# Mixers of a hybrid diffusion trunk: half-filled products on TensorE widened to 128 rows or 128 columns

## Chip, cores and metric

The kernel runs on one core of one Trainium2 chip. The metric is the device time of one execution in microseconds (us), the median over the runs.

## What is computed

One inference step of a trunk with two layers, shared by 512 latent tokens and 128 prompt tokens. Each layer is a half-step FFN, a mixer and a second half-step FFN, each behind an RMS norm with a modulation. The mixer has three parallel groups of heads: MLA (8 heads, softmax over all keys), a sliding window with grouped queries (SWA, 8 query heads on 2 key/value heads, a band of 128 to either side, cached context and a sink), and a gated delta net (GDN, 4 heads, in both directions, a scan over chunks of 64 tokens).

```python
def mixer_latent(h, lp, ctx):
    pr = project_mixers(h, lp)
    o_mla = mla_attend(q_nope, rope(q_rope), [kn_l, kn_c], [rope(krope), krope_c], [v_l, v_c])
    o_swa = swa_band_attend(rope(sq), rope(sk), sv, sk_c, sv_c, sink)
    o_gdn = gdn_bidirectional(pr, lp, st_fwd, st_bwd)
    return concat([o_mla, o_swa, o_gdn]) @ lp['w_out']

def gated_delta_step(s, w_i, u_i, qd_i, kd_i, a_i, gt_i):   # one chunk of 64 tokens
    v_new = u_i - w_i @ s
    o_i = qd_i @ s + a_i @ v_new
    s = s * gt_i + kd_i.T @ v_new                           # state, 128 x 128
```

## The kernel before

Activations lie with features on the partitions and the 640 tokens (512 latent, 128 prompt) along the row. Weighted products are made in float32r: every operand is split into a high and a low part, and a product is hi·hi + lo·hi + hi·lo; the rest of the mixer is in float32, where one product appears in the trace as two passes.

The program is a list of Python calls from which a tile framework makes one fixed order per engine, by a simulated timeline of its own (`schedule_with_timeline_sim`). At run time every engine works its list strictly in that order, and semaphores join the lists. So where the order of two engines isn't changed, a faster engine only meets its next wait earlier.

**Projections and GDN** (`mixer`, L316 on). `linear` (L93 to L108, products at L104) multiplies `h` by the weights of the mixers, three float32r products for each 128 features and each half of the 640 columns. Between these products the framework places the GDN of heads 0 to 3 (`gdn_group`, L592). Within a group, tokens lie in four pairs of chunks (u = 0 to 3), each pair on 128 partitions: chunk c on rows 64c to 64c+63. For each direction d POOL makes `kd` (L665, L666), the keys times the decay to the end of their chunk, `ekd` (from `gates`, L588). `step` (L729 to L740) is one chunk of the scan: L736 multiplies by the state (128 rows), L737 (DVE) puts the new values into the chunk's half of `UU`, and L739 makes the update of the state from that half:

```python
ps = slice(c * 64, c * 64 + 64)
nc.tensor.matmul(p2[:, :P], lhsT=KD_[d][ps, us], rhs=UU[d][ps, us], start=True, stop=True)
```

There are 16 such steps in a group, five groups in a layer (the fifth, for the prompt, is worked beside SWA) and two layers: 160.

**SWA** (`swa`, L939 to L1002). For each key/value head, `kh` (the high part of the keys) is loaded twice, into rows 0 to 63 and 64 to 127; `kl` (the low part) once, into rows 0 to 63; the values `vv` as [128, 6, 64]. `qh` holds the high part of the queries on rows 0 to 63 and the low part on rows 64 to 127. So one product of 128 rows gives hi·hi + lo·hi, and a second one of 64 rows hi·lo:

```python
for lh, rh in ((qh[:, q], kh[:, k0:k0 + w]), (qh[:64, q], kl[:64, k0:k0 + w])):
```

These alternate at L974: for each head four products for the first two blocks of queries, two for each of the others, and two for the prompt (L999). A mask product follows (L978), then `finish` (softmax: DVE, ACT, and POOL for the division, L899 to L909).

**Products with the values** (`pv`, L912 to L937; SWA and MLA). The probabilities are transposed on TensorE (L924), copied by ACT (L931), and multiplied at L935 with the values of one head as weights, 128 rows by 64 columns; the result lies on 64 partitions of PSUM and ACT copies it out (L937). SWA has 9 such products for each head, MLA 11.

**MLA** (`mla`, L1004 to L1043): keys and queries of 96 rows, scores at L1029, `vv` loaded for every head from `dv`, which `project` (L843 to L855) has written as [8 heads, 128, 6, 64]. After the first heads, the finished outputs are read back (`of`, L507) and split for the last product of the mixer.

Of the kernel before, what the change touches and what calls it, by code (L numbers as in the profile page):

```python
# [14 lines left out]
P = 128  # L15
# [26 lines left out]
class Net:  # L42
# [13 lines left out]
    def banks(self, **n):  # L56
        """psum tags and their banks, for the phase that opens"""
        side = {"side": n.pop("side")} if "side" in n else {}
        return _Banks(self, n, self.pool(self.nm("psum"), space=PSUM, reuse_waits="tile", **side))
# [12 lines left out]
    def move(self, dst, src):  # L72
        """between memories, of values that are float32r on either side"""
        raw = lambda x: x.bitcast(F32) if x.dtype == F32R else x
        self.nc.sync.dma_start(raw(dst), raw(src))
# [17 lines left out]
    def linear(self, ws, rhs, m=P, cols=HALVES, after={}):  # L93
        """for each column range: psum[:m, :n] = sum_k w[k]^T rhs[k], in three float32r products."""
        nc = self.nc
        ps = []
        kt = len(rhs)
        for c0, cw in cols:
            p = self.pt("L")
            ps.append(p)  # L100
            for k in range(kt):
                (wh, wl), (rh, rl) = ws[k], rhs[k]
                for n, (w, r) in enumerate(((wh, rh), (wl, rh), (wh, rl))):
                    i = nc.tensor.matmul(p[:m, :cw], lhsT=w[:, :m], rhs=r[:, c0:c0 + cw],  # L104
                                         start=(k == 0 and n == 0), stop=(k == kt - 1 and n == 2))
                    if (k, n) in after:
                        self.tc.add_manual_dep(i.ins, after[k, n].ins.name, mybir.DependencyInfo(mybir.DependencyClass.NoSync, mybir.DependencyReason.DATA), reason="norm")
        return ps  # L108

    def square(self, pool, xk, nfeat, bufs=3):  # L110
        """takes the squares (by the number of features) of one more tile of features"""
        nc = self.nc
        sq = pool.tile([P, T], F32, tag="sq", name=self.nm("sq"), bufs=bufs)
        for c0, cw in HALVES:
            nc.scalar.activation(sq[:, c0:c0 + cw], xk[:, c0:c0 + cw], AF.Square, scale=nfeat ** -0.5)
        self.addsquare(sq)
# [10 lines left out]
    def rstd(self, pool, kind="G", windows=(0, 128, 256, 384, 512), last=True):  # L127
        """by token (partition) and window of 128: 1/sqrt(mean(x^2) + eps) over the features squared so far"""
        nc = self.nc
        nb = len(windows)  # L130
        ps = self.pt(kind)
        r0, r = (pool.tile([P, nb], F32, tag="rs", name=self.nm("rs"), bufs=2) for _ in range(2))
        for i, t in enumerate(self.sq):
            for b, c in enumerate(windows):
                self.lastmm = nc.tensor.matmul(ps[:, 2 * b:2 * b + 2], lhsT=t[:, c:c + P], rhs=self.ones[:, :2],
                                               start=(i == 0 and b == 0), stop=(i == 1 and b == nb - 1))
        if last:
            self.sq = []
        nc.vector.tensor_scalar(r0, ps[:, :2 * nb].rearrange("p (b c) -> p b c", c=2)[:, :, 0], EPS, None, ALU.add)
        nc.gpsimd.tensor_tensor(r, r0, self.mhalf[:, :nb], ALU.pow)  # L140
        return r

    def spread(self, r, half, windows, kind="G"):
        """r [token, window] on every partition, tokens along the row: psum of a column half"""
# [36 lines left out]
    def addgate(self, k, ps, G, sq=None, half=None):  # L181
        """adds to the features k the gated columns of ps, and takes their squares"""
# [10 lines left out]
    def residual(self, k, w, rhs, G, squares):  # L193
        """x[k] += gate * (w^T rhs); after the last k the norm's factors of the first half of the columns
        are worked out beside the products of the second"""
# [52 lines left out]
    def adaln(self, l, i, start=False):  # L248
        """columns i*512 to (i+1)*512 of silu(cond) @ w_ada + b_ada, by feature and group: the sums over the
        blocks of 128 features on the vector engine and GpSimd and the rest on the tensor engine, or all there"""  # L250
# [42 lines left out]
    def fill(self, *after):  # L293
        """a job where the tensor engine has more to do than the others"""
# [5 lines left out]
    def rope(self, pool, z, np_, kind, mask):  # L300
        """rotate the latent columns of z in place"""
# [13 lines left out]
    def mixer(self, l, A, B, G):  # L315
# [17 lines left out]
        def parts(s, m=P, w=T):  # L333
            """hi and lo of s"""
# [4 lines left out]
        def put(d, hl):  # L339
            """latent and prompt columns into [latent, cache, prompt]"""  # L340
# [17 lines left out]
        # gates and the rotary key  # L358
# [9 lines left out]
        # gated delta-net: convolution, silu  # L368
# [6 lines left out]
        def prompt(n, hh, src):  # L375
            """the prompt's columns of a head, kept for the last group"""
# [32 lines left out]
        def window():  # L409
# [11 lines left out]
            # values by token: latent blocks, cache, prompt  # L421
# [126 lines left out]
    def gates(self, l, gp, pg):  # L548
# [9 lines left out]
        # softplus(y) = max(y, 0) + log1p(exp(-|y|)), log1p(e) = 2 atanh(e / (2 + e))  # L558
# [29 lines left out]
        self.egc, self.ekd, self.egt = ex[:, 0:40], ex[:, 40:80], (ex[:, 80:120], ex[:, 120:160])  # L588
# [3 lines left out]
    def gdn_group(self, l, g, qw, k, v, z):  # L592
        """g < 4: the latent tokens of head g, in four pairs of chunks; g == 4: the prompt, a pair of chunks by head."""
# [9 lines left out]
        # norms of k and q by token  # L603
# [22 lines left out]
        # natural layouts  # L626
# [9 lines left out]
        # K K^T and K Q^T  # L636
# [10 lines left out]
        for d in range(2):  # L647
# [17 lines left out]
            kd = t("kd", 3)  # L665
            nc.gpsimd.tensor_tensor(u4(kd), u4(kn), cols(self.ekd, d), ALU.mult)  # L666
            KD_.append(kd)
        # inverses of the 16x16 diagonal blocks of I+U (d=1 transposed: both are upper triangular)
# [57 lines left out]
        # scan over the chunks  # L726
        oq = [t("oq", 3) for _ in range(2)]

        def step(d, S, ci):  # L729
# [9 lines left out]
            nc.tensor.matmul(p2[:, :P], lhsT=KD_[d][ps, us], rhs=UU[d][ps, us], start=True, stop=True)  # L739
# [60 lines left out]
    def project(self, l, st, draw, tab32, pair):  # L800
# [24 lines left out]
        # keys: columns latent, cache, prompt  # L825
# [17 lines left out]
        self.dv = self.dram.tile([8, P, 6, 64], F32, tag=self.nm("dv"), name=self.nm("dv"))  # L843
        for b in range(6):
# [8 lines left out]
            t = cast("hd", [P, 8, 64])  # L853
            nc.scalar.activation(t, p.rearrange("p (h d) -> p h d", d=64), AF.Copy)
# [37 lines left out]
    def finish(self, S, scale, nscale, nsink, sink):  # L892
        """softmax weights of the score columns S [P, parts, columns], by row; scale: a number, or one by row"""
# [18 lines left out]
    def pv(self, blocks, vv, o, r0, c0, width):  # L912
        """blocks: list of (value block, [(probability tile, its column, output block)]);
        o[r0:r0+64, c0:c0+width] = sum over the value blocks."""
# [19 lines left out]
        for n, (vb, ti, s0, w, oc) in enumerate(place):  # L934
            nc.tensor.matmul(po[:64, oc:oc + w], lhsT=vv[:, vb, :], rhs=hl[ti][:, s0:s0 + w],  # L935
                             start=(n == 0), stop=(n == len(place) - 1))
        nc.scalar.activation(o[r0:r0 + 64, c0:c0 + width], po[:64, :width], AF.Copy)  # L937

    def swa(self, l):  # L939
        nc, att = self.nc, self.att  # L940
        sink = self.sm(l, 'sink')
        for kv in range(2):
            # columns: latent, cached context, prompt
            kh, kl = (att.tile([P, 768], F32R, tag="k", name=self.nm("k"), bufs=4) for _ in range(2))
            vv = att.tile([P, 6, 64], F32, tag="vv", name=self.nm("vv"), bufs=2)
# [3 lines left out]
            self.move(kl[:64], self.dsk[1][rows])  # L949
            self.move(vv, self.dsv[kv])  # L950
            for hh in range(4):
# [9 lines left out]
                def scores(n):  # L961
# [10 lines left out]
                    for o0, k0, w in rng:  # L972
                        for lh, rh in ((qh[:, q], kh[:, k0:k0 + w]), (qh[:64, q], kl[:64, k0:k0 + w])):
                            nc.tensor.matmul(p[:, o0:o0 + w], lhsT=lh, rhs=rh, start=(k == 0), stop=(k == last - 1))  # L974
                            k += 1
# [22 lines left out]
                for n, (lh, rh) in enumerate(((qh[:, TL:], kh[:, T:]), (qh[:64, TL:], kl[:64, T:]))):  # L998
                    nc.tensor.matmul(p[:, :P], lhsT=lh, rhs=rh, start=(n == 0), stop=(n == 1))  # L999
# [4 lines left out]
    def mla(self, l, heads, wp=None, osplit=None, hook=None):  # L1004
        nc, a, att = self.nc, self.a, self.att
        for head in heads:
# [12 lines left out]
            vv = att.tile([P, 6, 64], F32, tag="vv", name=self.nm("vv"), bufs=2)  # L1019
            self.move(vv, self.dv[head])  # L1020
            if head % 2 == 0:
                ot = (wp or att).tile([P, T], F32, tag="of" if wp else "out", name=self.nm("of"), bufs=2)
# [125 lines left out]
class _Banks:  # L1148
    """psum tags and their banks, as long as the context lasts"""
# [13 lines left out]
class _Bufs:  # L1163
    """a pool whose tags have their own number of buffers"""
# [38 lines left out]
def _layout(x):  # L1203
    """the inputs, laid out as the tiles that the program loads."""
    C = np.ascontiguousarray

    def tiles(w, k, n):
        """[L, K, N] -> [L, N/n, P, K/P, n]"""
# [9 lines left out]
    # q, k, v, z of the delta-net; sk, sv, sq; ckv, cq  # L1218
# [48 lines left out]
```

## Time and profile before

| | |
|---|---|
| median of 3 runs | 3419.33 us (3416.01 to 3420.2) |
| profiled execution | span 3412.5 us, which is all that the profile gives of its own time |
| runs above the span | 6.8 us |
| TensorE: busy, products / weight loads | 98% / 91% |
| DVE, ACT, POOL busy | 55%, 41%, 13% |
| granted clock, mean | 0.987 |

The span runs from the first to the last instruction of one profiled execution. Busy shares of TensorE are of modelled ends of pipelined products, so that how fast it goes is read from the distance between the starts of its instructions, in the timeline. A layer's mixer stands at 556 to 1246 us and at 2237 to 2925 us; the stages used below are the scans of GDN heads between the projections (to about 912 and 2594 us), SWA with the prompt's GDN group (to 1046 and 2728), and MLA (to 1161 and 2839).

### The profile page before, as it was taken

What the parts mean: (1) busy time and instruction counts of PE and PEld (TensorE: products, weight loads), DVE (VectorE), ACT (ScalarE), POOL (GpSimd) and SP (SyncE); (2) the same over time, 40 slices, a digit from 0 to 9 for tenths busy, and PEclk for the clock granted to TensorE, in tenths of its full rate; (3) what the DMA queues carried; (4) which work ended last, traced back from release to release, by engine and by line L of the source; (5) the groups of instructions that cost most, each with busy time, mean ns of one, the idle gap of its engine ahead of it and who ended that gap; (6) DMA issues with size and microseconds to landing.
All of it is one profiled execution on the core that took longest, in us unless ns stands there. A gap on an engine that the chain in (4) does not pass through costs nothing.

```text
span 3412.5 us, 56739 instructions
## 1 busy us (share of the span) xinstructions
PE 3356.0 (98%) x22036; PEld 3112.9 (91%) x22036; DVE 1880.6 (55%) x4353; ACT 1387.8 (41%) x3041; POOL 429.8 (13%) x460
## 2 busy tenths in 40 slices
PE   8999999999999999999999999999999999999998
PEld 5999999999866799999999999999997668999998
DVE  4574677676765345643346745477777553433333
ACT  3332335544565533322233323264455563322222
POOL 0010011211333200000000100012113341000000
PEclk9999999999999999999999999999999999999999
DMA  5353453222514223432224524323143142222222
GB/s 210 125 156 109 145 167 106 92 74 90 170 45 123 85 87 120 149 107 77 66 90 142 164 97 137 102 86 107 65 130 125 49 136 80 75 71 74 80 67 76
DMA packets 181470, 363.21 MB, mean 106 GB/s; under 512 B 34256, under 2 KB 70736, under 8 KB 181200
## 3 DMA queue, kind: packets, MB, share of 16 engines
q1 hardware_dynamic: 181200, 359.58, 32.9%
q8 instruction: 173, 2.83, 0.3%
q14 instruction: 97, 0.79, 0.1%
HBM read 313.46 MB, written 46.04 MB: 105 GB/s over the span
## 4 chain that ended last, share of the span: by engine, by line
PE 92%; DVE 4%; DMA 2%; ACT 1%; issue 1%; SPq 0%; POOL 0%; POOLq 0%; DVEq 0%; ACTq 0%
PE psL L104 71%; PE psT L935 4%; PE psG L697 3%; PE psT L924 2%; PE psS L739 2%; PE psS L974 2%; PE psS L1029 1%; PE psS L736 1%; PE psG L275 1%; DVE hf L169 1%; DMA of<-do 1%; PE psS L770 1%; PE psL L852 1%; DMA adaw<-in_wada_dram 0%; PE psG L610 0%
## 5 line engine op out<-in xcount | busy, mean ns | idle before, releaser
L70 DVE TENSOR_TENSOR wlo<-wr,whi 128x512 fp32r<-128x512 f32 (+2 forms) x726 | 495.0, 683 | 709.2 <-ACT whi L67 707.2
L67 ACT ACTIVATE whi<-wr 128x512 fp32r<-128x512 f32 (+2 forms) x726 | 446.3, 616 | 883.2 <-PE psL L104 622.2
L104 PE MATMUL psL<-hb,whi 128*128 128x320 f32 x1968 | 523.3, 313 | 1.1 <-DVE hb L171 1.1
L104 PE MATMUL psL<-hc,whi 128*128 128x320 f32 x1952 | 519.4, 313 | 0.4 <-DVE hc L171 0.4
L104 PE MATMUL psL<-ha,whi 128*128 128x320 f32 x1856 | 492.5, 312 | 5.3 <-DVE ha L171 4.0
L104 PE MATMUL psL<-hd,whi 128*128 128x320 f32 (+1 forms) x1856 | 486.8, 310 | 3.5 <-DVE hd L171 3.5
L104 PE MATMUL psL<-mh,wlo 128*128 128x320 f32 x1408 | 434.2, 309 | 0.0
L104 PE MATMUL psL<-ml,whi 128*128 128x320 f32 x1408 | 434.0, 309 | 0.0
L104 PE MATMUL psL<-mh,whi 128*128 128x320 f32 x1408 | 432.9, 310 | 0.0
L104 PEld LDWEIGHTS psL<-hb,whi 128*128 128x128 f32 x1968 | 351.1, 189 | 4.7 <-DVE hb L171 2.3
L104 PEld LDWEIGHTS psL<-hc,whi 128*128 128x128 f32 x1952 | 348.0, 189 | 3.1 <-DVE hc L171 1.0
L104 PEld LDWEIGHTS psL<-ha,whi 128*128 128x128 f32 x1856 | 329.7, 188 | 10.1 <-DVE ha L171 5.9
L104 PEld LDWEIGHTS psL<-hd,whi 128*128 128x128 f32 (+1 forms) x1856 | 328.6, 187 | 8.1 <-DVE hd L171 5.2
L269 DVE SCALAR_TENSOR_TENSOR ada<-adaw,cs,ada 128x512 f32<-128x512 f32 x448 | 313.6, 743 | 0.0
L104 PE MATMUL psL<-hb,wlo 128*128 128x320 f32 (+1 forms) x984 | 307.0, 312 | 0.0
L104 PE MATMUL psL<-hc,wlo 128*128 128x320 f32 (+1 forms) x976 | 305.2, 313 | 0.0
L104 PE MATMUL psL<-hd,wlo 128*128 128x320 f32 (+1 forms) x928 | 287.8, 310 | 0.0
L104 PE MATMUL psL<-ha,wlo 128*128 128x320 f32 (+1 forms) x928 | 287.7, 311 | 0.0
L104 PEld LDWEIGHTS psL<-ml,whi 128*128 128x128 f32 x1408 | 264.0, 188 | 2.8
L104 PEld LDWEIGHTS psL<-mh,whi 128*128 128x128 f32 x1408 | 263.5, 188 | 3.0
L104 PEld LDWEIGHTS psL<-mh,wlo 128*128 128x128 f32 x1408 | 264.1, 188 | 2.0
L188 DVE SCALAR_TENSOR_TENSOR x<-psL,G,x 128x320 f32<-128x320 f32 (+2 forms) x240 | 97.8, 435 | 231.3 <-PE psL L104 231.0
(298 smaller groups left out, 5591.2 us busy)
## 6 DMA issues: line engine op xcount, KB each, us to landing
adaw<-in_wada_dram SPq DMA_DIRECT2D x288, 256.0 KB, 2.9
wr<-in_w1a_dram SPq DMA_DIRECT2D x88, 512.0 KB, 3.6
wr<-in_w1b_dram SPq DMA_DIRECT2D x88, 512.0 KB, 3.5
wr<-in_win_dram SPq DMA_DIRECT2D x54, 512.0 KB, 3.5
wr<-in_w2a_dram SPq DMA_DIRECT2D x32, 512.0 KB, 4.0
wr<-in_w2b_dram SPq DMA_DIRECT2D x32, 512.0 KB, 3.5
wr<-in_wo_dram SPq DMA_DIRECT2D x16, 512.0 KB, 3.6
dqn<-hd SPq DMA_DIRECT2D x24, 320.0 KB, 2.7
```

Source lines behind the costliest of these rows:

```text
L67: self.nc.scalar.activation(dst, src, AF.Copy)
L70: self.nc.vector.tensor_tensor(dst, src, hi.bitcast(F32), ALU.subtract)
L104: i = nc.tensor.matmul(p[:m, :cw], lhsT=w[:, :m], rhs=r[:, c0:c0 + cw], start=(k == 0 and n == 0), stop=(k == kt - 1 and n == 2))
L169: nc.vector.scalar_tensor_tensor(t[:, c0:c0 + n], self.x[k][:, s], A[:, k, g:g + 1], r[j][:, c0:c0 + n], ALU.mult, ALU.mult)
L188: i = self.nc.vector.scalar_tensor_tensor(xs, ps[j][:, c0:c0 + n], G[:, k, g:g + 1], xs, ALU.mult, ALU.add)
L269: nc.vector.scalar_tensor_tensor(acc[g], raw, c, acc[g], ALU.mult, ALU.add)
L275: nc.tensor.matmul(ps[:2, :], lhsT=self.sel[:, g, :], rhs=x, start=(g + n == 0), stop=(g + n == 2))
L697: nc.tensor.matmul(p[:, s], lhsT=lhs[:, s], rhs=rhs[:, s], start=True, stop=True)
L739: nc.tensor.matmul(p2[:, :P], lhsT=KD_[d][ps, us], rhs=UU[d][ps, us], start=True, stop=True)
L924: nc.tensor.transpose(pt[:, used:used + P], pr[:, pc:pc + P], self.ident)
L935: nc.tensor.matmul(po[:64, oc:oc + w], lhsT=vv[:, vb, :], rhs=hl[ti][:, s0:s0 + w], start=(n == 0), stop=(n == len(place) - 1))
L974: nc.tensor.matmul(p[:, o0:o0 + w], lhsT=lh, rhs=rh, start=(k == 0), stop=(k == last - 1))
```

## The change

No product is left that uses only 64 rows or 64 columns in these three places:

- **State update.** `gates` makes two `ekd`, each zero on the rows of the other chunk; POOL makes two `kd` for each direction (buffers 3 to 6), and the update multiplies all 128 rows. The other chunk's rows meet zeros.
- **Scores of SWA.** `kl` is loaded into both halves, and both products have 128 rows. The second one now also adds lo·lo.
- **Values.** In MLA `vv` holds two heads side by side, [128, 6, 128], loaded once for two heads, and `dv` is written as [4, 128, 6, 128]; in SWA both halves are loaded with the same values. The product has 128 columns, and ACT copies out the 64 partitions of its head.

```diff
@@ gates
-        self.egc, self.ekd, self.egt = ex[:, 0:40], ex[:, 40:80], (ex[:, 80:120], ex[:, 120:160])
+        self.egc, self.egt = ex[:, 0:40], (ex[:, 80:120], ex[:, 120:160])
+        self.ekd = []
+        for c in range(2):
+            e = t(f"ekd{c}", 40)
+            nc.vector.tensor_tensor(e, ex[:, 40:80], self.mat[('blka', 'blkb')[c]][:, 0:1].to_broadcast([P, 40]), ALU.mult)
+            self.ekd.append(e)
...
@@ gdn_group
-            kd = t("kd", 3)
-            nc.gpsimd.tensor_tensor(u4(kd), u4(kn), cols(self.ekd, d), ALU.mult)
+            kd = [t("kd", 6) for _ in range(2)]
+            for c in range(2):
+                nc.gpsimd.tensor_tensor(u4(kd[c]), u4(kn), cols(self.ekd[c], d), ALU.mult)
...
-            nc.tensor.matmul(p2[:, :P], lhsT=KD_[d][ps, us], rhs=UU[d][ps, us], start=True, stop=True)
+            nc.tensor.matmul(p2[:, :P], lhsT=KD_[d][c][:, us], rhs=UU[d][:, us], start=True, stop=True)
...
@@ project
-        self.dv = self.dram.tile([8, P, 6, 64], F32, tag=self.nm("dv"), name=self.nm("dv"))
+        self.dv = self.dram.tile([4, P, 6, P], F32, tag=self.nm("dv"), name=self.nm("dv"))
...
-            t = cast("hd", [P, 8, 64])
-            nc.scalar.activation(t, p.rearrange("p (h d) -> p h d", d=64), AF.Copy)
+            t = cast("hd", [P, 4, P])
+            nc.scalar.activation(t, p.rearrange("p (h d) -> p h d", d=P), AF.Copy)
...
@@ pv
-            nc.tensor.matmul(po[:64, oc:oc + w], lhsT=vv[:, vb, :], rhs=hl[ti][:, s0:s0 + w],
+            nc.tensor.matmul(po[:, oc:oc + w], lhsT=vv[:, vb, :], rhs=hl[ti][:, s0:s0 + w],
                              start=(n == 0), stop=(n == len(place) - 1))
-        nc.scalar.activation(o[r0:r0 + 64, c0:c0 + width], po[:64, :width], AF.Copy)
+        nc.scalar.activation(o[r0:r0 + 64, c0:c0 + width], po[r0:r0 + 64, :width], AF.Copy)
...
@@ swa
-            vv = att.tile([P, 6, 64], F32, tag="vv", name=self.nm("vv"), bufs=2)
+            vv = att.tile([P, 6, P], F32, tag="vv", name=self.nm("vv"), bufs=2)
...
-            self.move(kl[:64], self.dsk[1][rows])
-            self.move(vv, self.dsv[kv])
+                self.move(kl[half], self.dsk[1][rows])
+                self.move(vv[:, :, half], self.dsv[kv])
...
-                        for lh, rh in ((qh[:, q], kh[:, k0:k0 + w]), (qh[:64, q], kl[:64, k0:k0 + w])):
-                            nc.tensor.matmul(p[:, o0:o0 + w], lhsT=lh, rhs=rh, start=(k == 0), stop=(k == last - 1))
+                        for x in (kh, kl):
+                            nc.tensor.matmul(p[:, o0:o0 + w], lhsT=qh[:, q], rhs=x[:, k0:k0 + w], start=(k == 0), stop=(k == last - 1))
...
-                for n, (lh, rh) in enumerate(((qh[:, TL:], kh[:, T:]), (qh[:64, TL:], kl[:64, T:]))):
-                    nc.tensor.matmul(p[:, :P], lhsT=lh, rhs=rh, start=(n == 0), stop=(n == 1))
+                for n, x in enumerate((kh, kl)):
+                    nc.tensor.matmul(p[:, :P], lhsT=qh[:, TL:], rhs=x[:, T:], start=(n == 0), stop=(n == 1))
...
@@ mla
-            vv = att.tile([P, 6, 64], F32, tag="vv", name=self.nm("vv"), bufs=2)
-            self.move(vv, self.dv[head])
             if head % 2 == 0:
+                vv = att.tile([P, 6, P], F32, tag="vv", name=self.nm("vv"), bufs=2)
+                self.move(vv, self.dv[head // 2])
```

The number of TensorE's products stays the same, and so does their order up to SWA, but for some transposes and norms that stand a few places from where they stood. From L585 on, lines of the changed kernel are 5 to 7 higher: the update of the state is L745, the scores L981 and L1006, the values L942, `kd` L672.

In each block of rows below, numbers after `_` are the program's own and move with every added tile. The first place is SP's queue at the start of SWA in the first layer; `k` are the two key tiles, `q` the queries of a head, `v` an operand of the prompt's GDN group. Before:

```order
L75 DMA k_10484<-dsk_7256 64x768 x2
L75 DMA k_10485<-dsk_7257 64x768
L75 DMA vv_10486<-dsv_7343 128x384
L478 DMA v_9490<-d_992_5811 128x512
L75 DMA q_10492<-dsq_7503 64x640
L75 DMA q_10492<-dsq_7504 64x640
```

and with the change:

```order
L75 DMA k_10508<-dsk_7268 64x768
L75 DMA k_10509<-dsk_7269 64x768
L75 DMA vv_10510<-dsv_7355 128x6x64
L478 DMA v_9510<-d_994_5815 128x512
L75 DMA k_10508<-dsk_7268 64x768
L75 DMA k_10509<-dsk_7269 64x768
L75 DMA vv_10510<-dsv_7355 128x6x64
L75 DMA q_10518<-dsq_7515 64x640
L75 DMA q_10518<-dsq_7516 64x640
```

Two more loads stand ahead of the first queries.

The second place is TensorE's list at the same point (L736 and L739, now L742 and L745, are the last head's scan; L610 and L629, now L615 and L634, open the prompt's GDN group; L974, now L981, are the first scores). Before:

```order
L736 MATMUL psS_1635_9038<-st_9034,wqb_8455 128x128
L974 MATMUL psS_10495<-k_10484,q_10492 128x256
L974 MATMUL psS_10495<-k_10485,q_10492 128x256
L974 MATMUL psS_10495<-k_10484,q_10492 128x128
L974 MATMUL psS_10495<-k_10485,q_10492 128x128
```

and with the change:

```order
L742 MATMUL psS_1645_9058<-st_9054,wqb_8471 128x128
L615 MATMUL psG_9517<-ones,QK_9518 128x2 x4
L615 MATMUL psG_9517<-ones,QK_9524 128x2 x4
L634 MATMUL psG_9543<-mats,k_9509 128x128 x4
L745 MATMUL psS_1645_9058<-uu_9035,kd_8841 128x128
L981 MATMUL psS_10521<-k_10508,q_10518 128x256
L981 MATMUL psS_10521<-k_10509,q_10518 128x256
```

Thirteen products of GDN now stand ahead of the first scores.

The third place is POOL's list in the scan of head 0, where the second direction's `kd` of head 1 stands (`pad` are the zero borders for a convolution, cleared by POOL). Before:

```order
L388 MEMSET pad_8673 128x2
L388 MEMSET pad_8673 128x4
L388 MEMSET pad_8673 128x2
L666 TENSOR_TENSOR kd_6936<-kn_6878,gex_5793 128x512
L756 MEMSET st_9776 128x128
```

and with the change:

```order
L672 TENSOR_TENSOR kd_6946<-kn_6886,ekd_962_5795 128x512
L672 TENSOR_TENSOR kd_6947<-kn_6886,ekd_963_5797 128x512
L388 MEMSET pad_8689 128x2
L388 MEMSET pad_8689 128x4
L388 MEMSET pad_8689 128x2
L762 MEMSET st_9800 128x128
```

One `pad` is now cleared behind the two `kd`, no longer ahead of the one.

## Rows read from the trace of the kernel before

**Rows 1.** The chain that ended last: share of the span by engine.
```profile
PE 92%; DVE 4%; DMA 2%; ACT 1%; issue 1%; SPq 0%; POOL 0%; POOLq 0%; DVEq 0%; ACTq 0%
```

**Rows 2.** Busy us by stage: stretch and length, PE, PEld, DVE, ACT, POOL, PEclk, DMA.
```profile
660.00:850.00 190.00, 189.58 (x1326) 179.15 (x1325) 130.53 (x364) 89.51 (x218) 35.67 (x50) 0.98 0.25 82
912.00:1046.00 134.00, 133.82 (x742) 92.20 (x742) 84.25 (x331) 82.07 (x253) 46.58 (x53) 0.97 0.20 58
1046.00:1161.00 115.00, 107.89 (x570) 74.19 (x570) 54.99 (x140) 71.79 (x172) 44.53 (x41) 0.94 0.41 125
2594.00:2728.00 134.00, 133.16 (x745) 91.83 (x744) 86.97 (x335) 82.33 (x253) 47.17 (x55) 0.99 0.20 58
2728.00:2839.00 111.00, 104.99 (x569) 72.64 (x569) 56.34 (x140) 71.47 (x172) 44.04 (x41) 0.97 0.43 131
```

**Rows 3.** Busy us of L739 alone ahead of SWA: PE (xpasses), PEld.
```profile
660.00:912.00 252.00, 23.52 (x96) 14.32 (x96) 0.98 0.35 112
```

**Rows 4.** TensorE's timeline around one L739: start us, us, what, xpasses.
```profile
888.90 0.31 PE L104 MATMUL psL<-hb,wlo 128*128 128x320 f32 x1
889.05 0.31 PE L104 MATMUL psL<-hb,whi 128*128 128x320 f32 x1
889.29 0.49 PE L739 MATMUL psS<-uu,kd 64*128 64x128 f32 x2
889.70 0.41 PE L104 MATMUL psL<-hc,whi 128*128 128x320 f32 x1
889.95 0.31 PE L104 MATMUL psL<-hc,wlo 128*128 128x320 f32 x1
```

**Rows 5.** The same view around one L736, of equal shape but 128 rows.
```profile
694.67 0.31 PE L104 MATMUL psL<-hb,whi 128*128 128x320 f32 x1
694.82 0.38 PE L736 MATMUL psS<-st,wqb 128*128 128x128 f32 x2
694.95 0.39 PE L104 MATMUL psL<-hb,whi 128*128 128x320 f32 x1
695.18 0.31 PE L104 MATMUL psL<-hb,wlo 128*128 128x320 f32 x1
```

**Rows 6.** The same view: scores of two blocks of queries, and the masks behind.
```profile
957.43 1.30 PE L974 MATMUL psS<-k,q 128*128 128x384 f32 x4
958.67 0.28 PE L978 MATMUL psS<-bmsw,identb 128*128 128x128 bf16 x2
...
961.05 0.93 PE L974 MATMUL psS<-k,q 128*128 128x512 f32 x2
961.91 0.29 PE L978 MATMUL psS<-bmsw,identb 128*128 128x128 bf16 x2
```

**Rows 7.** The same view in MLA: values (L935) between scores.
```profile
1129.46 1.12 PE L1029 MATMUL psS<-k,q 96*128 96x320 f32 x6
1130.51 1.08 PE L935 MATMUL psT<-pt,vv 128*64 128x256 f32 x4
1131.52 0.33 PE L924 MATMUL psT<-mats,pr 128*128 128x128 f32 x1
1131.60 1.12 PE L1029 MATMUL psS<-k,q 96*128 96x320 f32 x6
1132.65 0.65 PE L935 MATMUL psT<-pt,vv 128*64 128x256 f32 x2
```

**Rows 8.** Groups of weight loads by shape: xcount, busy us, mean ns, idle before.
```profile
L935 PEld LDWEIGHTS psT<-pt,vv 128*64 128x64 f32 x640 | 74.1, 137 | 52.3 <-issue 8.6 <-ACT pt L931 7.6 <-ACT pr L904 1.5
L739 PEld LDWEIGHTS psS<-uu,kd 64*128 64x128 f32 x320 | 46.6, 187 | 26.5 <-issue 8.4 <-ACT pr L904 2.0 <-ACT den L906 1.3
```

**Rows 9.** POOL's groups: `kd`, mean ns of one, and what POOL waited for.
```profile
L666 POOL TENSOR_TENSOR kd<-kn,gex 128x512 f32<-128x512 f32 x20 | 22.0, 1106 | 99.1 <-PE psS L739 82.0 <-ACT bd L704 15.3 <-ACT kn L631 1.8
```

**Rows 10.** SP's timeline: issues of the first SWA keys.
```profile
903.63 1.79 SPq L75 DMA_DIRECT2D k<-dsk  x3
```

**Rows 11.** A piece of the chain in MLA: start us, us, what.
```profile
1074.79 4.73 DMA of<-do
```

## Prediction

> **What bounds the kernel now.** I read the chain of waits first: 92% of it is TensorE's work [rows 1], so every nanosecond taken from TensorE's list counts wherever TensorE doesn't wait. Then the busy times by stage, to see where that holds. While the scans of heads 0 to 3 run between the projections, and in SWA, TensorE is busy for all but a fraction of a microsecond of the stage (189.6 of 190, 133.8 of 134), and DVE and ACT for some 60 to 70% of it; in MLA TensorE falls short of its stage by 6 to 7 us [rows 2]. Busy ends are modelled, though, so the third view is the timeline, where the distance between starts tells what a product costs. Here the three edited products stand out.
>
> *State update.* In a stream of full products (one each 0.15 us, 888.90 to 889.05) the two passes of L739, on 64 rows, start 0.24 us after the product ahead of them. The next full one starts 0.41 us later, and the one after it 0.25 us later: 0.90 us from the last full product ahead to the second behind [rows 4]. L736, of the same kind and columns on 128 rows, passes through the same stream in 0.51 us (694.67 to 695.18) [rows 5]. So the half-height update is the dearer one, by 0.39 us: it is paid when TensorE goes to it, between its own passes, and when it returns.
>
> *Scores.* Four products, in turn of 128 and 64 rows, take 1.24 us (957.43 to 958.67), and a pair of 512 columns 0.86 us [rows 6]. By the column, a full product of 320 columns at 0.15 us [rows 4] gives about 0.24 us for 512 columns and 0.18 for 384 (estimates), and the 128-column ones lie below 0.15.
>
> *Values.* Six scores of 96 rows with 320 columns take 1.05 us between two runs of L935 [rows 7], where six full products at 0.15 would take 0.88 to 0.90. So the price of going to L935's 64 columns and back sticks to its neighbours too, while 96 rows cost nothing extra: six at 0.15 fit but for that price.
>
> **The change part by part.**
>
> *State update, removed cost.* 320 passes [rows 8] are 160 updates. Ahead of SWA there are 96 passes in the first layer [rows 3], and the second layer runs the same program: 96 updates, mostly among full products, at 0.38: 36 us. The other 64 stand in the SWA stage, often beside L935 or L974, where entry and exit are shared; bounds 0.28 (own passes and one edge: 0.41 less 0.13) and 0.39, I take 0.36: 23 us.
>
> *Scores, removed cost.* A set of four goes from 1.24 to about 0.58 (0.18 + 0.18 + 0.11 + 0.11), a saving of 0.66; a pair of 512 from 0.86 to 0.47, a saving of 0.39. For each head there are two sets of four, two long pairs and the prompt's short pair (taken at half a set, 0.33): 2.4 us. Sixteen heads: 38 us. Bounds: with 0.15 for every short product 34, with 0.08 42.
>
> *Values, removed cost.* 640 passes [rows 8], mostly four in a run [rows 7]: some 160 runs. The six scores show 0.15 to 0.17 us of it (one entry and the second product after a return); the exit itself adds about 0.09, by the entry of L739 [rows 4]. I take 0.25 us a run, bounds 0.15 and 0.39: 40 us (24 to 62). With 9 products a head in SWA and 11 in MLA, 18 us of it lie in SWA and 22 in MLA.
>
> *Sum on TensorE:* 36 ahead of SWA, 23 + 38 + 18 = 79 in SWA, 22 in MLA, 137 in all.
>
> *What of it reaches the end.* Ahead of SWA, DVE (130.5 of 190) and ACT have room [rows 2], the order is the same, and TensorE hardly waits: 90%, 33 us. In SWA each layer's 134 us would become 94; DVE has 84 to 87 us of work there and ACT 82 [rows 2], in chains (maximum, exponential, division, transpose, copy) through two PSUM banks for scores and two for the rest. Both at 90% is more than such chains give. I take 72%, 57 us: each stage about 106 us, with DVE and ACT near 80%. What is late next there is a softmax, not a product. In MLA TensorE waits already, and the chain runs through read-backs of finished heads of up to 4.7 us each [rows 11]; half, 11 us.
>
> *What it adds.* Twenty more `kd` on POOL at 1.1 us [rows 9]. POOL is busy 36 of 190 us there [rows 2]; the cover is its idle time. But it waits in order: it has spent 82 us waiting for a scan to release a `kd` buffer [rows 9], and a `pad` now stands behind two such `kd` where it stood ahead of one. That can hold the pad's convolution on DVE, and weights behind it, by one scan step and two `kd`, some 5 us; DVE has room, so I take nothing, bounds 0 and 10 over both layers. At SWA's start two more loads, at 0.6 us to issue [rows 10], stand ahead of the first queries: 1.2 us later in each layer; thirteen GDN products were moved ahead of the scores and cover about that. I take 3 us for both layers with the slower strided load of `vv`, bounds 0 and 7. In MLA eight loads fewer of `vv`, hidden before: nothing. Two small multiplications more on DVE in `gates`: below 1 us, nothing. ACT copies the same 64 partitions: nothing.
>
> *Sum.* 33 + 57 + 11 - 3 = 98 us. The profiled span of 3412.5 us becomes 3314.5; the runs' median lies 6.8 us above the span, so **3321 us**.
>
> **The rivals.**
>
> *Wider weight loads (slower than forecast).* The values' loads go from 64 to 128 columns: 137 ns now, 187 ns for 128 columns [rows 8], 50 ns more for each of 640. If none is hidden, 32 us come back: 3353 us. Against it: L736's two passes, with loads as wide, need 0.13 us to the next product's start [rows 5], less than one load takes, so that loads run under products. The Trainium skill ("TensorE: Matmul & The Clock Gate", LDWEIGHTS) says that the time of a load goes by columns and not by rows; the trace agrees (187 ns on 64 rows, 137 at half the columns), and the rule speaks against the third part of the change alone.
>
> *The others hold the softmax stages.* DVE, ACT and the read-backs set the length of SWA and MLA as soon as TensorE is quicker; only the 33 us ahead of SWA are left: 3386 us. For it: DVE and ACT at 65% in SWA, two banks each. Against it: TensorE waits under 1 us in 134 [rows 2], so the others now run ahead of it.
>
> *The price isn't one of size.* It stays with the products when they are filled, because of the places where they stand or their operands: 3412 to 3426 us, no difference. Against it: L736 stands in the same places and doesn't pay [rows 5]. The Trainium skill ("TensorE: Matmul & The Clock Gate", "Why this matters for your kernels") would come out near here: a product over a few rows takes the same time as one over 128, and small ones only gain by running side by side. By it neither update nor scores would save anything, and the sum would be 24 us from the values, 3395 us. Rows 4 and 5 contradict it for 64 rows: 0.39 us apart.
>
> *Slower: the clock.* The granted clock is 0.94 to 0.99 in the two stages [rows 2], the lowest in MLA, where TensorE waits most. If quicker products turn into waits and the clock falls, all else there is slower. After the gain the stages hold about 106 and 109 us in a layer, 430 in both, at about 0.97. At clock c they need 430 x 0.97 / c: the gain of 98 us is eaten at c = 0.79, and at 0.70 the kernel takes 3321 + 166 = 3487 us. Against it: the clock is 0.97 and more in SWA, with its present chains.
>
> **How the numbers follow.** Forecast 0.77; wider loads 0.08; softmax stages 0.07; no difference 0.04; clock 0.04. The range: all 137 us arrive and nothing is added, 3282, which I cut to 3286, since no stage has ever all of it; at the other end 80% ahead of SWA (29), 40% in SWA (32), nothing in MLA and 10 us added, 51 us, 3368. It takes in the wider loads. About 0.2%, 7 us, is what a measurement of this kernel can tell from no change: faster 0.92 (the first three), same 0.04, slower 0.04.
>
> **What would show it.** Right: L745 passes through its stream in about 0.5 us like L736, with 128 rows; a set of four scores takes about 0.6 us; six scores of MLA beside values 0.9; SWA shrinks from 134 to about 106 us in each layer and MLA by some 5, with more waits of TensorE for ACT and POOL there than now; the stage ahead of SWA by 16 a layer. Wrong: L942 starts further apart than L935's passes do; SWA stays above 120 us with TensorE waiting; the sandwich of rows 4 keeps its 0.9 us; the granted clock in SWA falls below 0.9.

## The result, and the profile after

The changed kernel takes **3324.52 us** (median of 4 runs, 3323.15 to 3325.07), the kernel before on the same chip 3417.67: a ratio of 0.9729, 95% interval 0.9715 to 0.9743. It is faster, 3.5 us above the forecast and inside the range.

The profiled span went from 3412.5 to 3323.3 us. The chain is still TensorE's, but less so than in [rows 1]:

```profile
PE 87%; DVE 6%; ACT 3%; DMA 2%; issue 2%; SPq 0%; POOL 0%; POOLq 0%; DVEq 0%; ACTq 0%
```

Busy us by stage after, the view of [rows 2] (stretch and length, PE, PEld, DVE, ACT, POOL, PEclk, DMA). The stages begin at the first SWA score (896 and 2532 us), the first MLA score (1007 and 2642) and end with the last product with values (1113 and 2749):

```profile
660.00:850.00 190.00, 189.19 (x1423) 186.75 (x1423) 144.75 (x397) 103.55 (x257) 44.23 (x57) 1.00 0.30 99
896.00:1007.00 111.00, 104.02 (x720) 91.95 (x720) 87.03 (x326) 80.47 (x251) 46.07 (x54) 0.97 0.28 73
1007.00:1113.00 106.00, 94.15 (x567) 84.55 (x567) 52.98 (x138) 70.70 (x172) 43.85 (x41) 0.95 0.46 135
2532.00:2642.00 110.00, 101.79 (x716) 89.47 (x716) 88.03 (x332) 79.76 (x250) 48.30 (x56) 0.98 0.29 76
2642.00:2749.00 107.00, 94.59 (x565) 84.06 (x565) 51.85 (x132) 70.79 (x171) 42.85 (x40) 0.95 0.46 133
```

In the same 190 us ahead of SWA TensorE now does 1423 passes instead of 1326; the clock there is 1.00 where it was 0.98 [rows 2], so that some 4 us of the gain in the first layer (190 x 0.02, an estimate) are the clock's and not the change's. SWA went from 134 to 111 and 110 us, MLA from 115 and 111 to 106 and 107. Against the ends in [rows 2] the saving by stage is 16 + 14 us ahead of SWA, 23 + 24 in SWA, and 8 + 3 in MLA (8.3 and 3.4 by the unrounded start of the first score and end of the last product): the 89 us by which the span is shorter, but for rounding. The work of DVE and ACT in SWA and MLA is within 5 us of what it was, while TensorE, idle for 0.2 and 0.8 us of the two SWA stages before and for 6 to 7 of the MLA stages, is now idle for 7 to 8 and for 12.

TensorE's timeline, the places that answer to [rows 4] and [rows 6] (start us, us, what, xpasses):

```profile
870.20 0.31 PE L104 MATMUL psL<-hb,whi 128*128 128x320 f32 x1
870.35 0.38 PE L745 MATMUL psS<-uu,kd 128*128 128x128 f32 x2
870.49 0.39 PE L104 MATMUL psL<-hc,whi 128*128 128x320 f32 x1
870.72 0.30 PE L104 MATMUL psL<-hc,wlo 128*128 128x320 f32 x1
...
908.07 0.77 PE L981 MATMUL psS<-k,q 128*128 128x384 f32 x4
908.68 0.28 PE L985 MATMUL psS<-bmsw,identb 128*128 128x128 bf16 x2
...
923.73 0.71 PE L981 MATMUL psS<-k,q 128*128 128x512 f32 x2
924.28 0.29 PE L985 MATMUL psS<-bmsw,identb 128*128 128x128 bf16 x2
...
1090.72 1.03 PE L942 MATMUL psT<-pt,vv 128*128 128x256 f32 x4
1091.39 1.23 PE L1036 MATMUL psS<-k,q 96*128 96x320 f32 x6
1092.46 1.03 PE L942 MATMUL psT<-pt,vv 128*128 128x256 f32 x4
1093.33 0.27 PE L931 MATMUL psT<-mats,pr 128*128 128x128 f32 x1
```

From the last full product ahead to the second one behind, the update takes 0.52 us where it took 0.90. Four scores take 0.61 instead of 1.24, a pair of 512 columns 0.55 instead of 0.86. In MLA four values and six scores take 1.74 us together, where [rows 7] has 1.05 + 1.01 = 2.06.

Groups of weight loads after (view of [rows 8]):

```profile
L942 PEld LDWEIGHTS psT<-pt,vv 128*128 128x128 f32 x640 | 113.6, 196 | 35.3 <-ACT pt L938 22.9 <-ACT of L944 0.2 <-issue 0.2
L745 PEld LDWEIGHTS psS<-uu,kd 128*128 128x128 f32 x320 | 51.4, 191 | 4.8 <-ACT oq L744 3.6
```

The values' loads are longer, 196 ns instead of 137, and still hidden: the four passes from 1092.46 take 0.87 us, less than the 1.01 before. What TensorE waited for in the first layer's MLA after (us in total, times, longest), and one row of ACT's waits in the same stage, first before the change and then after:

```profile
PE psT L942 <- ACT pt L938: 5.6, 6, 2.9
PE psS L1036 <- ACT pr L910: 3.9, 2, 2.1
PE psT L931 <- ACT pt L938: 3.6, 2, 2.9
```

```profile
ACT oh L67 <- DMA of<-do: 1.5, 3, 0.8
```

```profile
ACT oh L67 <- DMA of<-do: 7.6, 4, 2.5
```

ACT stands 7.6 us for read-backs that its list has ahead of other work, and TensorE waits 9.2 us for ACT's copies `pt`. In the kernel before the same row of ACT was 1.5 us. In the second layer the difference is smaller, 4.9 us before and 7.1 after.

### The profile page after: what moved, and what is told of

The parts are those of the page before. It is cut to its first block, busy times and chain, and to the rows that moved or that the text cites. A ratio compares the mean times of both kernels' runs of the same rounds, so it can differ in the third digit from the quotient of the medians.

```text
span 3323.3 us, 56733 instructions
## 1 busy us (share of the span) xinstructions
PE 3241.5 (98%) x22036; PEld 3129.5 (94%) x22036; DVE 1886.3 (57%) x4357; ACT 1384.8 (42%) x3041; POOL 452.2 (14%) x480
## 4 chain that ended last, share of the span: by engine, by line
PE 87%; DVE 6%; ACT 3%; DMA 2%; issue 2%; SPq 0%; POOL 0%; POOLq 0%; DVEq 0%; ACTq 0%
PE psL L104 72%; PE psT L942 3%; PE psG L703 3%; PE psS L1036 2%; PE psT L931 1%; PE psG L275 1%; PE psS L742 1%; DMA of<-do 1%; PE psS L745 1%; ACT pr L910 1%; PE psS L981 1%; DVE hf L169 1%; DMA adaw<-in_wada_dram 0%; DVE wlo L70 0%; PE psS L776 0%
## 5 line engine op out<-in xcount | busy, mean ns | idle before, releaser
L273 POOL TENSOR_TENSOR adal<-ada,adah 128x512 fp32r<-128x512 f32 x64 | 89.8, 1404 | 1041.7 <-ACT adah L67 823.3
```

Of the source, the lines that this page charges most:

```text
L273: nc.gpsimd.tensor_tensor(lo, acc[g], hi.bitcast(F32), ALU.subtract)
```

## Experiments

Each was timed beside the kernel before, whose medians were 3418.0 to 3419.6 us. A gain or loss against the changed kernel is taken from medians of runs on different chips or at different times, and the intervals of the two ratios (some 4 to 6 us to either side) go with it; differences of 5 to 12 us are therefore read from the stages too.

**The three parts alone.** The kernel before, with one part of the diff above in each.

```diff
e1:  only gates, kd and the update (L745)
e2:  only kl in both halves and the scores (L981, L1006)
e3:  only dv, vv, the values and their copy (L942, L944)
```

> The kernel before with the first part of the change alone (two kd, update on 128 rows). Theory: every half-size product costs its change of size, and in the full change the softmax chains gave a part of it back because all three parts fell on the same stage. Alone, this part meets no such limit: 30 us ahead of SWA and some 20 of 23 in SWA, so about 3368 us. Rival, nothing is given back and each part brings its share of what the full change brought (30 us ahead of SWA, 47/79 of 23 in SWA): about 3374 us. By the theory the three parts alone add up to clearly more than the 93 us of the whole (107 or more), by the rival to 93.

Measured: 3368.45 us, ratio 0.9856 (0.9839 to 0.9873), 51 us.

> The kernel before with the second part alone (kl in both halves, both score products on 128 rows). Theory: alone it brings nearly all of its 38 us, 33 or so, since TensorE hardly waits in SWA before: about 3385 us. Rival, it brings 47/79 of 38, 23 us: about 3395 us. If a product's rows did not matter at all: 3418 us.

Measured: 3385.04 us, 0.9900 (0.9875 to 0.9925), 34 us.

> The kernel before with the third part alone (values of 128 columns). Theory: 15 of 18 us in SWA and 11 to 13 in MLA, about 3391 us. Rival, wider weight loads are exposed as soon as no other gap covers them: 32 us less, 3423 us, no gain. Rival, each part brings its share of the whole: 11 + 13 us, 3394 us.

Measured: 3401.03 us, 0.9949 (0.9930 to 0.9969), 18 us.

The sum is 103 us, the whole 93; with 6 to 9 us of uncertainty on each part this doesn't tell the theory from its rival. The stages say more. From the first SWA score to the first MLA score, SWA is shorter by 4 + 6 us in e1, 13 + 15 in e2 and 8 + 3 in e3: 49 us alone, 47 together. So by length of stage the parts did not take each other's gain in SWA, against my theory of giving back.

The total of e1 came as expected, but not its split: 17 + 19 us ahead of SWA instead of 30, some of them the clock's (1.00 from 660 to 850 us, 0.98 before), and 10 in SWA instead of 20. The premise that this part meets no limit alone is what failed. The two SWA stages of e1 (columns as above):

```profile
895.00:1026.00 131.00, 128.24 (x743) 92.54 (x744) 87.26 (x332) 81.57 (x252) 48.29 (x55) 0.96 0.20 58
2550.00:2678.00 128.00, 126.13 (x729) 90.54 (x730) 85.39 (x327) 81.58 (x252) 48.89 (x55) 0.96 0.20 58
```

TensorE is idle for 2.8 and 1.9 us where it was for 0.2 and 0.8, and the clock is 0.96 where it was 0.97 and 0.99 [rows 2]. At the shares before, 131 x 0.01 + 128 x 0.03 = 5 us would come back (an estimate); with the 4 us of idle time that makes 19 us of TensorE's time in SWA, not 10.

The values came out low in e3 for a like reason, the clock in the second layer (SWA, then MLA):

```profile
2581.00:2712.00 131.00, 127.55 (x711) 97.17 (x711) 87.04 (x331) 80.97 (x251) 43.85 (x52) 0.94 0.22 60
2712.00:2820.00 108.00, 97.24 (x565) 86.56 (x565) 52.40 (x132) 70.87 (x171) 42.87 (x40) 0.92 0.44 132
```

Before, the two were at 0.99 and 0.97. Full shares of the clock would be worth 131 x 0.05 + 108 x 0.05 = 12 us. All four runs of e3 had a mean clock of 0.982 to 0.984. This is an estimate, not an experiment.

**Which products pay.** The changed kernel with 96 rows in the second score:

```diff
- lhsT=qh[:, q], rhs=x[:, k0:k0 + w]
+ lhsT=qh[:96 if x is kl else P, q], rhs=x[:96 if x is kl else P, k0:k0 + w]
```

> The changed kernel with the second score product on 96 rows instead of 128; it adds only half of the lo times lo terms. Theory: the price belongs to products on 64 rows or fewer, and 96 rows count as full, as the scores of MLA (96 rows) beside transposes (128 rows) suggest: 3325 us, no change. Rival, any change of the number of rows from one product to the next costs: the 38 us of the scores come back as far as they are felt, 3345 to 3355 us.

Measured: 3324.71 us, ratio 0.9726 (0.9708 to 0.9744): no difference from the change. Unequal heights as such cost nothing; 64 rows do.

**Per pass or per change of size.** Each update issued twice, before (e5) and after (e6):

```diff
+ for _ in range(2):
      nc.tensor.matmul(p2[:, :P], lhsT=KD_..., rhs=UU..., start=True, stop=True)
```

> The kernel before with each 64-row update of the state issued twice in a row, with the same result. Theory: besides entry and exit, each of its passes costs 0.21 us, as its weight load on 64 rows is not hidden: 160 x 2 x 0.21 = 67 us more, 3485 us, less what SWA hides. Rival, only the change of size costs, and a pass among its like takes the 0.11 us of a full one: 160 x 2 x 0.11 = 35 us more, 3453 us.

> The changed kernel with each 128-row update issued twice in a row, with the same result: the counterpart of the half-height one issued twice. Theory: 160 x 2 x 0.11 = 35 us more on TensorE, of which the 20 to 22 ahead of SWA arrive and of the 14 in SWA about half, as TensorE waits there: 3324 + 28 = 3352 us. Rival, TensorE sets the end everywhere: 3360 us. Rival, TensorE has slack in both stages: under 3340 us.

Measured: e5 3447.23 us, 1.0077 (1.0062 to 1.0092), 28 us more than before; e6 3354.97 us, 0.9804 (0.9790 to 0.9819), 30 us more than the change. TensorE's timeline of e5:

```profile
884.56 0.31 PE L104 MATMUL psL<-hb,whi 128*128 128x320 f32 x1
884.80 0.71 PE L740 MATMUL psS<-uu,kd 64*128 64x128 f32 x4
885.43 0.42 PE L104 MATMUL psL<-hc,whi 128*128 128x320 f32 x1
885.69 0.31 PE L104 MATMUL psL<-hc,wlo 128*128 128x320 f32 x1
```

Four passes need 0.63 us, two needed 0.41 [rows 4]: the two more cost 0.11 each, as full ones do (by the starts of the single passes 0.21, 0.11, 0.11 and 0.20). My theory of 0.21 a pass falls. A half-height product pays on the way in, once behind its first pass and on the way out, and nothing for further passes. The Trainium skill ("TensorEngine Tiling (Array Packing)", Key Properties) says that a change of tiling mode drains TensorE; the trace agrees in that the price is paid at the change, and its size, 0.39 us in this stream, is the trace's.

**What holds MLA after the change.** Three edits of the changed kernel, and one of the kernel before:

```diff
e7:  copies pt (L938) of MLA
- nc.scalar.activation(f[:, :used], p[:, :used], AF.Copy)
+ nc.vector.tensor_copy(f[:, :used], p[:, :used])
e8 (after), e9 (before), e12 (after, 8):  read-backs
- tag="of", ... bufs=2
+ tag="of", ... bufs=4
e10: high part of a read-back
- self.hi(hi, f)
+ nc.vector.tensor_copy(hi, f)
```

> The changed kernel with the copies of the transposed probabilities in MLA on DVE instead of ACT. Theory: in MLA TensorE now waits mostly for ACT (its copies stand behind other work in ACT's list), and DVE is busy for only half of the stage; the waits of some 19 us in a layer fall by 3 to 8: 3309 to 3319 us. Rival, the read-backs or the division hold the stage: 3325 us, no change. Rival, DVE's reductions now stand behind the copies: slower, up to 3335 us.

Measured: 3337.02 us, 0.9750 (0.9734 to 0.9766), 12 us slower than the change by the medians, 7 by the ratios, whose intervals overlap. MLA alone takes 0.6 and 4.7 us more; another 5 us lie ahead of the first SWA score, which the edit doesn't touch, and why stays open. ACT's row in the first layer's MLA, first after the change, then in e7:

```profile
ACT pr L910 <- DVE nb L909: 12.7, 12, 2.6
```

```profile
ACT pr L910 <- DVE nb L909: 32.9, 19, 3.4
```

In MLA the last rival came: the maximum and its scaling now stand behind copies on DVE, and ACT's exponentials wait for them.

> The changed kernel with four instead of two buffers for the outputs read back in MLA. Theory of the prediction, that the read-backs hold MLA: its chain loses up to 2 of the 4.7 us reads in each layer, 3316 to 3321 us. Rival, the chain of softmax and copies holds it: 3325 us, no change.

Measured: **3311.31 us**, 0.9683 (0.9667 to 0.9699), 13 us faster than the change, more than expected. Both MLA stages, and ACT's row in the first:

```profile
1010.00:1109.00 99.00, 91.95 (x564) 82.74 (x563) 51.55 (x136) 71.00 (x169) 45.17 (x41) 0.97 0.48 144
2635.00:2734.00 99.00, 92.42 (x565) 82.96 (x564) 52.36 (x132) 71.46 (x171) 42.91 (x40) 0.97 0.49 144
...
ACT oh L67 <- DMA of<-do: 2.9, 2, 1.6
```

MLA takes 99 us instead of 106 and 107, ACT's wait falls from 7.6 to 2.9 us, and the clock is 0.97 instead of 0.95.

> The kernel before with four instead of two buffers for the outputs read back in MLA, which brought 13 us on top of the change. Theory: that wait is one that the change uncovered, since ACT stood 1.5 us for read-backs in the first layer's MLA before the change and 7.6 us after it: before the change the buffers bring less, 0 to 6 us, 3413 to 3419 us. Rival, the buffers are a separate improvement that was there all along: 3406 us, 13 us again.

Measured: 3422.27 us, 1.0024 (1.0007 to 1.0041): nothing gained, rather 0.07 to 0.41% lost. What is lost goes with the clock: at the same mean clock of 0.985 five executions of e9 took 3415.8 to 3422.2 us and six of the kernel before 3416.7 to 3420.4. ACT's row for read-backs in the two MLA stages of e9 is 3.6 and 5.1 us, no less than before. So the 13 us are not an improvement that was there all along. That read-backs became a limit only when TensorE got quicker fits this, but isn't shown by it, since here the buffers did not shorten the wait.

> The changed kernel, with two buffers as it has them, but the copy that makes the high part of a read-back on DVE instead of ACT. Theory: the read-backs cost time because ACT waits for them in its list (7 us in a layer) and the copies of the transposed probabilities stand behind it; with that wait out of ACT's list most of the 13 us that four buffers brought come, 3312 to 3318 us. Rival, it is the buffers or SP's queue that hold, whoever makes the copy: 3325 us, no change. Rival, DVE's reductions now stand behind the read-backs instead: 3328 to 3340 us.

Measured: 3318.12 us, 0.9713 (0.9700 to 0.9725), 6 us faster than the change, about half of what the buffers bring. ACT has no row for read-backs in MLA any more, and MLA takes 102 and 103 us. So ACT's place in the list is part of the mechanism, and not all of it.

> The changed kernel with eight buffers for the read-backs of MLA. Theory: four buffers already took ACT's wait for read-backs from 7 to 3 us in a layer and gave 13 us; eight take the rest of the wait and hold what was won: 3305 to 3311 us. Rival, the 13 us came from the order that the framework happened to make with four, not from the buffers: with eight the time falls back towards the two-buffer version, 3316 to 3325 us.

Measured: 3312.36 us, 0.9691 (0.9678 to 0.9704), as with four. The gain stays with another order of the program, and the further gain that I expected of eight did not come. e8 and e12 are the quickest versions of this study.

**What holds SWA after the change.** `finish` without the last line for SWA, which leaves SWA's outputs undivided:

```diff
+ if nsink is None:
      nc.gpsimd.tensor_tensor(pr, pr, den[:, 0:1].to_broadcast([P, w]), ALU.mult)
```

> The changed kernel without POOL's division of the probabilities by their sum in SWA, which leaves the outputs of SWA undivided. Theory of the prediction, that a softmax chain is what is late next in SWA: each chain is shorter by a division, and of the 17 to 18 us of gaps that TensorE has in each SWA stage 3 to 6 go: 3312 to 3319 us. Rival, the gaps come from DVE's and ACT's own queues and the lower clock behind each gap, and the division lies beside other work: 3325 us, no change.

Measured: 3317.76 us, 0.9707 (0.9695 to 0.9720), 7 us faster than the change. The two SWA stages:

```profile
899.00:1004.00 105.00, 101.71 (x723) 91.49 (x723) 78.18 (x323) 80.03 (x251) 11.93 (x13) 0.97 0.30 79
2531.00:2635.00 104.00, 97.96 (x712) 87.79 (x713) 80.87 (x324) 79.58 (x250) 13.35 (x14) 1.00 0.29 77
```

They are shorter by 6 us each, 12 in all, of which 5 are lost again elsewhere (3 ahead of the first score and 2 in the first MLA, in the profiled execution). Some 2 us in the second layer (104 x 0.02, an estimate) go with its higher clock. The chain through the division does hold a part of SWA.

## Why the prediction was right, and where its terms were not

*The price is one of size: right.* The update's passage shrank from 0.90 to 0.52 us (forecast 0.5), a set of four scores from 1.24 to 0.61 (0.6). e1 shows the part alone (51 us), e4 that 96 rows don't pay, e5 that the price is paid for the change of size and not for each pass. "Between its own passes" has to read: behind the first pass only. The rule that a product over few rows takes as long as one over 128 (the Trainium skill, "TensorE: Matmul & The Clock Gate", "Why this matters for your kernels") would have given 3395 us; e2, which changes rows alone, brought 34 us where it would give none.

*Ahead of SWA: 33 forecast, 30 measured.* From 660 to 850 us TensorE is busy for 189.2 of 190, and none of its waits ahead of SWA is for POOL, so the second `kd` was covered, as assumed. Some 4 of the 30 us are the clock's, as said above; that is luck.

*SWA: 57 forecast, 47 measured.* The two steps, a gross of 79 us and a share of 72%, can be told apart only in part. TensorE is idle for 15 us of the two stages where it was idle for 1, so its own work there shrank by at least 47 + 14 = 61 us. Busy time hides some more: in the trace TensorE stops 25 times in each stage after the change and twice before, the pass ahead of a stop counts as busy some 0.16 us longer than it would hold up the next one, and the first float32 pass behind a stop, at 128 columns, takes 0.21 us to the next start instead of 0.11. At 0.26 us for 46 stops that is 12 us, 73 in all (an estimate). Some 6 of these us are work that no longer lies in the stages, the products moved ahead of the scores above all: by the rows the two have 22 and 29 passes fewer, at 0.11 each (an estimate). So the gross was too large, by 6 to 24 us; 47 of 61 to 73 is 64 to 77%, and the share may have held. By length of stage all three terms came short alone: the update 10 of 23 us, the scores 28 of 38, the values 11 of 18. Idle time and clock account for most of what the update and the values lack (e1, e3).

The update's price itself was not too high. In SWA many of its neighbours are float32 products, and there it is the same as in [rows 4]. Before, and then after:

```profile
2668.29 0.48 PE L739 MATMUL psS<-uu,kd 64*128 64x128 f32 x2
2668.70 0.71 PE L770 MATMUL psS<-uu,A 128*128 128x128 f32 x4
2669.25 1.95 PE L697 MATMUL psG<-TT,U 128*128 128x128 f32 x16
```

```profile
972.80 0.39 PE L745 MATMUL psS<-uu,kd 128*128 128x128 f32 x2
973.02 0.49 PE L931 MATMUL psT<-mats,pr 128*128 128x128 f32 x3
```

Two full passes take 0.22 us, 0.11 each. The two half-height ones and the way out take 0.41, and the four full passes behind them 0.55 instead of 0.44: 0.30 us, and 0.09 for the way in (taken from [rows 4]) make 0.39. So among float32 products each of the two changes of size costs about 0.19 us, 0.09 where it happens and 0.10 behind the first pass after it. To the start of the next product alone the update would seem to cost 0.28. Where the neighbour is itself a product of 64 rows or columns, as L935 often is, a change is shared; how many of the 64 updates save that way was not counted. Which term of the 79 us was too large stays open.

"A softmax is late next there" is right in part for SWA: without the division it falls to 105 and 104 us. "106 us, DVE and ACT near 80%" became 111 and 110 us, with 78 to 80 and 73%.

*MLA: 11 forecast, 12 measured.* TensorE is idle there for 24 us instead of 13, so its work shrank by at least 12 + 11 = 23 us where 22 had been forecast, and about half of it arrived: both steps held. "Six scores in 0.9" holds too, though the starts hide it. From their first start to the next values the scores seem to take 1.07 us, but that start stands 0.67 us behind the start of four value passes that need 0.87 (1092.46 to 1093.33); of the 1.74 us of both, 0.87 is left for the scores. A run and its scores together save 0.32 us, above the 0.25 taken. Read-backs hold most of the other half: with four buffers (e8) MLA gives 13 us more.

*What it adds: 3 forecast.* The first scores wait 1.4 us for queries in the first layer and 0.7 in the second; it lies within SWA's sum.

*The sum.* 98 us forecast, 89 measured in spans. The forecast lies nearer than that because 6.8 us were put on top of the span, where the profiled execution after lies 1.2 us below the median: by spans alone 3314.5 stands against 3323.3. That is luck. Every run listed takes 1.7 to 1.9 us longer than its own span; the other 5 of the 6.8 us are only that the profiled execution before was quicker than the median.

*Rivals.* Wider loads: no, the four passes of values take 0.87 us with loads of 196 ns. Softmax stages hold everything: no, SWA and MLA gave 59 us, but waits for DVE, ACT and read-backs keep a part of the rest. Clock: 0.95 to 0.98 in the stages, and by length and clock of each row 16 us lie in slow stretches before and after (134 x 0.03 + 115 x 0.06 + 134 x 0.01 + 111 x 0.03 against 111 x 0.03 + 106 x 0.05 + 110 x 0.02 + 107 x 0.05). Over the whole execution the mean is 0.987 before and after. It did not decide.

## To carry to other kernels

Price a half-filled product by what the stream around it loses, from the last full product ahead to the second one behind. Read only to the start of the first one behind, the update seemed to cost 0.28 us among float32 products; read to the second it cost 0.39, as among float32r ones, once for each visit however many passes it makes. Then ask what the stage does with the time: alone, the update brought 10 of its 23 us in SWA, where idle time and a lower clock took most of the rest. Where the engine that bounds the kernel gets quicker, look for loads that another engine's list has ahead of what the bound engine needs: two more buffers were worth 13 us after the change and nothing before it.

## What had not been expected of the hardware

The granted clock can fall to half while TensorE counts as busy throughout. In the profiled execution of e9 (10 us each; columns as above):

```profile
2690.00:2700.00 10.00, 10.00 (x51) 6.18 (x50) 5.76 (x21) 6.52 (x21) 3.73 (x4) 1.00 0.04 10
2700.00:2710.00 10.00, 10.00 (x36) 5.91 (x37) 3.93 (x15) 3.92 (x13) 1.23 (x3) 0.65 0.04 14
2710.00:2720.00 10.00, 10.00 (x30) 6.05 (x29) 3.08 (x15) 4.06 (x12) 2.08 (x2) 0.50 0.02 2
2720.00:2730.00 10.00, 10.00 (x34) 6.87 (x33) 3.27 (x12) 3.66 (x14) 1.22 (x2) 0.50 0.18 65
```

That SWA stage took 150 us at a mean clock of 0.85. The executions of e9 spread from 3412.52 us (clock 0.987) to 3441.98 (0.979). Behind a real wait it falls too; after the change, in MLA:

```profile
1055.00:1060.00 5.00, 2.02 (x15) 1.51 (x13) 3.89 (x6) 1.63 (x4) 0.76 (x1) 1.00 0.23 66
1060.00:1065.00 5.00, 4.38 (x17) 3.79 (x18) 1.52 (x5) 3.25 (x10) 2.46 (x2) 0.66 0.00 0
```

TensorE was busy for 2.02 of 5 us at the full 2.4 GHz, and in the next 5 us it was granted 0.66 of it, so that part of them ran at 1.2. What starts the first kind of fall was not tried.
